# First mixer of a two-block transformer: order by hand up to the queries, compression before the decays, its additions on GpSimd

## Chip, core and metric

The kernel runs on one core of a Trainium2 chip. The metric is the device time of the whole program in microseconds; the time before is the median of three runs. TensorE is called PE, VectorE DVE, ScalarE ACT, GpSimd POOL, and SyncE, whose queue carries most DMAs, SP.

## The reference, cut to what matters

```python
def reference(x, ...):                       # x [1, 256, 1024] float32
    x = first_block(x, ...)
    return second_block(x, ...)

def first_block(x, ...):                     # one layer
    z = rms_norm(h, attn_norm) @ w_in        # 2856 columns
    nq, nkv, ngate, gq, gk, gv, glr, gout = split(z)
    o_nsa = nsa_mixer(nq, nkv, ngate, ...)   # 8 heads of 64, 2 key groups
    o_gla = gla_mixer(gq, gk, gv, glr, gout, ...)   # 4 heads, keys 64, values 128
    h = h + concat([o_nsa, o_gla]) @ w_out
    u = causal_dwconv(rms_norm(h, ffn_norm) @ w_up, conv_w, conv_b)
    gate, up = split(u)                      # 2816 each
    return h + (silu(gate) * up) @ w_down

def compress(t, pe, w1, w2):                 # in nsa_mixer, for keys and for values
    tb = t[:, blk] + pe[:, None, :]          # 15 blocks of 32 tokens, a new one every 16
    return gelu(tb.reshape(..., 32 * 64) @ w1) @ w2

# nsa_mixer: o = g0 * attention over the 15 compressed blocks
#              + g1 * attention over the selected blocks + g2 * attention in a window
# gla_mixer: linear attention with decay: log_a = log_sigmoid(glr @ w_gate2 + b) / 16,
#            q * exp(b), k * exp(-b), states carried over 4 chunks of 64 tokens,
#            rms_norm(o) * silu(gout)

def second_block(x, ...):                    # conv and attention mixer, then
    h = h + hier_moe(rmsnorm(h, norm2_g), w_group, w_router, w1, w3, w2)
                                             # 64 experts of 1024 x 512, two for each token
```

All operands are float32. The change touches only the first mixer (`nsa_mixer`, `gla_mixer` and the products by `w_in` that feed them) and the load of the router's weights.

## The kernel before

**Products.** PE has no fast float32 product, so each float32 matrix is split in two parts: `split` copies it into a rounded hi part (ACT, L154) and subtracts this from the original for the lo part (DVE, L155). A product is then three matmuls per piece: hi by hi, lo by hi, hi by lo. `tokmm` (L278) gives tokens by columns from pieces of 128 rows by 512 columns, `featmm` (L288) columns by tokens. Both take x turned, multiplied by the norm's gain and split (`gained_T`: transposes by PE at L241, xh by ACT at L246, xl by DVE at L247). The norm's factor per token, `rstd_of` (ACT L258, then small DVE steps of a Newton iteration at L220 to L222), is multiplied in behind the products.

**Weights.** `load_raw` (L122) brings them by SP in blocks of 1 MB into four raw buffers used in rotation, the halves of `low_61` and `low_62`; `load_k` makes two blocks of 512 columns, `load_c` one of 256. A raw buffer is loaded again when its last reader is done: the splits, and for the compression's weights, which are used as they are, PE. The split parts go through six pairs of buffers.

**Stages, in the program's order.** x is loaded (L187) between the two halves of the columns `w_cmp` that feed the compression (L181), turned, and multiplied by `w_cmp` (into cT), `w_q` (48 matmuls at L278, into qg), `w_kv` (48, into kg and vv), `w_gg` (the gates, 24 small ones), `w_gqk` (96, into qt and kt_), `w_gv` (48) and, later, `w_go` (48). Between them stand small chains: `gl` (DVE L383, the gate input) goes through a small product at L399, an exponential and a logarithm (ACT L401 to L403) and a running sum (PE L409) to the decays `e0`, `e1`, `e2` (ACT, and POOL at L419 and L422), which DVE multiplies into qt, kdT (L466) and kt_.

**Compression.** `sel`, eight matmuls at L502, spreads cT over partitions; ACT copies the result to `cd`; sixteen additions of 64x8x15 elements (DVE L510) add the position weights and write `tb`; 128 small matmuls (L518) multiply `tb` by `cmp_w1`; then a GELU, a transpose (L523), small products by `w2c` (L531, L534), and for the keys a norm and a rotation on DVE (`kcd`, L554). In the program it stands behind the decays and the loads of `w_gv`.

**The attention.** From L650 on: three score products for each of four head pairs (L654, L667), row maxima (DVE L627), exponentials (ACT), scalings (DVE L635), turned blocks (PE L641) and products by the values (L662, L675). PE's other products fill its waits.

**What sets the order.** A planner orders each engine's instructions; each engine then works in that order, and waits where an operand is missing. `tc.manual_schedule` keeps the written order instead, for the engines named. PSUM has three buffers for products (`pf`), two small ones (`pc`), two for transposes (`pt`) and one more (`po`).

**Later stages.** From 176 us a gated feed-forward layer with convolution, then the second block's mixer; from about 600 us the experts' weights, 402 MB, stream through buffers while PE multiplies them.

## Time and profile before

| | |
|---|---|
| median of three runs | 1534.73 us (1533.23 to 1536.35) |
| the profiled execution | 1533.03 us, of it the span 1531.2 us; mean granted clock 0.943 |
| busy in the span | PE 88%, DVE 39%, ACT 27%, POOL 8% |
| chain that ended last | DMA 50%, PE 44%, DVE 3% |
| moved | 502 MB, 328 GB/s over the span |

The profile is of one execution. Its timeline has a line for each run of like instructions: when they start, how long they take together, the engine, the line of the program, what is written and read, and in brackets how long the engine stood idle before and what it waited for. A view by stretches adds busy times between two moments. The chain that ended last is followed back from the last instruction to whatever released each step.

### The profile page before, as it was taken

To read this page: it belongs to the slowest core of one execution; us is meant where nothing else is said; L and a number is where in the kernel's file an instruction comes from. 1 tells how busy PE (TensorE), PEld (TensorE's weight loads), DVE (VectorE), ACT (ScalarE), POOL (GpSimd) and SP (SyncE) were. 2 spreads that over 40 slices of the span, in tenths; PEclk is the share of its full clock that TensorE was granted. 3 is DMA by queue.
4 is the path that set the end of the run, shared out by engine and by line. 5 is a ranking of instruction groups with operands and counts; after the bars stand their busy time and mean duration, and the time that the engine had idled before them with its cause. 6 is when DMAs were issued, how large, how long until landed. Compare 5 with 4: busy or idle time off the path is not lost.

```text
span 1531.2 us, 24384 instructions
## 1 busy us (share of the span) xinstructions
PE 1353.7 (88%) x10353; PEld 882.5 (58%) x10353; DVE 601.7 (39%) x1309; ACT 413.4 (27%) x734; POOL 126.8 (8%) x126
## 2 busy tenths in 40 slices
PE   7999999999999998999888888897887888887886
PEld 6766899998899996544343333343333433433332
DVE  5787777767876555322121121211211211111111
ACT  5455666555555443111001000010100000010001
POOL 3100032221212222000000000000000000000000
PEclk9999999999999999999898998988988899889998
DMA  9351666553545568999999999999999999999996
GB/s 322 127 189 56 206 207 216 170 193 121 172 159 202 184 237 345 396 424 426 426 427 426 427 427 425 427 425 427 427 427 427 425 428 425 428 426 426 426 425 246
DMA packets 113376, 502.39 MB, mean 328 GB/s; under 512 B 9825, under 2 KB 70770, under 8 KB 86002
## 3 DMA queue, kind: packets, MB, share of 16 engines
q1 hardware_dynamic: 110322, 499.66, 81.4%
q8 instruction: 83, 1.36, 0.4%
q10 hardware_dynamic: 2944, 1.16, 0.3%
q14 instruction: 27, 0.22, 0.0%
HBM read 499.74 MB, written 1.05 MB: 327 GB/s over the span
## 4 chain that ended last, share of the span: by engine, by line
DMA 50%; PE 44%; DVE 3%; SPq 1%; ACT 1%; issue 1%; POOL 0%; DVEq 0%; ACTq 0%
DMA w<-in_w 28%; DMA low<-in_w 21%; PE pf L288 11%; PE pf L870 8%; PE ps L1278 5%; PE pf L278 5%; PE acc L859 4%; PE oacc L1310 3%; PE ps L1300 1%; DMA low<-in_w_in 1%; PE acc L278 1%; PE ps L1211 1%; PE pc L1033 0%; PE pc L1010 0%; PE oacc L1315 0%
## 5 line engine op out<-in xcount | busy, mean ns | idle before, releaser
L1278 PE MATMUL ps<-w,xg 128*32 128x256 f32 x2896 | 287.5, 458 | 98.7 <-DMA w<-in_w 97.8
L1278 PEld LDWEIGHTS ps<-w,xg 128*32 128x32 f32 x2896 | 133.1, 130 | 218.0 <-DMA w<-in_w 114.2
L1310 PE MATMUL oacc<-y,swT 128*128 128x512 f32 (+1 forms) x516 | 237.3, 602 | 0.6 <-DVE y L229 0.4
L1289 DVE TENSOR_TENSOR ar<-ps,a 64x128 f32<-64x128 f32 x128 | 48.8, 382 | 443.9 <-ACT a L1284 443.1
L1278 PE MATMUL ps<-low,xg 128*32 128x256 f32 x1200 | 156.6, 481 | 47.0 <-DMA low<-in_w 46.2
L1310 PEld LDWEIGHTS oacc<-y,swT 128*128 128x128 f32 x516 | 92.6, 189 | 119.2 <-issue 117.4
L1284 ACT ACTIVATE a<-ps 64x256 f32<-64x256 f32 x64 | 24.0, 375 | 507.6 <-PE ps L1278 507.6
L229 DVE COPY y<-ps 128x512 f32<-128x512 f32 x64 | 44.3, 692 | 213.8 <-PE ps L1300 213.8
L1278 PEld LDWEIGHTS ps<-low,xg 128*32 128x32 f32 x1200 | 68.9, 136 | 102.2 <-DMA low<-in_w 53.4
L1300 PE MATMUL ps<-w,aT 128*32 128x512 f32 x696 | 86.5, 598 | 1.4 <-issue 1.4
L1262 ACT ACTIVATE swT<-ps 128x256 f32<-128x256 f32 x64 | 24.5, 383 | 211.4 <-PE ps L1260 211.4
L1211 PEld LDWEIGHTS ps<-oh,h3m 128*128 128x128 f32 x512 | 61.0, 195 | 26.7 <-issue 26.7
L1211 PE MATMUL ps<-oh,h3m 128*128 128x128 f32 x512 | 67.1, 285 | 1.0 <-DVE oh L1203 1.0
L227 ACT ACTIVATE y<-ps 128x512 f32<-128x512 f32 (+1 forms) x65 | 38.4, 590 | 108.4 <-PE ps L1300 108.3
L1213 DVE TENSOR_TENSOR xg<-ps,par 128x512 f32<-128x512 f32 x32 | 22.1, 692 | 69.6 <-PE ps L1211 69.6
L901 POOL TENSOR_TENSOR g<-uc,uc 128x256 f32<-128x256 f32 x22 | 31.7, 1439 | 160.2 <-ACT uc L899 151.5
L1300 PEld LDWEIGHTS ps<-w,aT 128*32 128x32 f32 x696 | 18.7, 109 | 40.2 <-issue 33.3
L1300 PE MATMUL ps<-low,aT 128*32 128x512 f32 x312 | 40.4, 598 | 1.0 <-DMA low<-in_w 1.0
L1253 DVE TENSOR_SCALAR sw<-cst,rk,Wm 128x128 f32<-128x128 f32 x128 | 38.1, 340 | 2.3 <-PE ps L1260 2.3
L1260 PEld LDWEIGHTS ps<-ident,sw 128*128 128x128 f32 x128 | 17.9, 141 | 33.5 <-issue 33.5
L155 DVE TENSOR_TENSOR w_downl<-low,w_downh 128x1024 fp32r<-128x1024 f32 x22 | 27.1, 1231 | 24.7 <-ACT w_downh L154 24.7
L859 PE MATMUL acc<-w_downh,gh 128*128 128x512 f32 x88 | 34.9, 397 | 0.0
(536 smaller groups left out, 2289.9 us busy)
## 6 DMA issues: line engine op xcount, KB each, us to landing
w<-in_w SPq DMA_DIRECT2D x119, 2048.0 KB, 39.4
low<-in_w SPq DMA_DIRECT2D x51, 2048.0 KB, 39.4
low<-in_w_in SPq DMA_DIRECT2D x36, 1024.0 KB, 5.0
w<-in_w SPq DMA_DIRECT2D x30, 1024.0 KB, 9.4
low<-in_w_up SPq DMA_DIRECT2D x22, 1024.0 KB, 5.2
low<-in_w SPq DMA_DIRECT2D x12, 1024.0 KB, 10.3
low<-in_w_down SPq DMA_DIRECT2D x11, 1024.0 KB, 5.1
low<-in_w_out SPq DMA_DIRECT2D x4, 1024.0 KB, 7.9
```

The lines of the kernel that those rows point to most:

```text
L227: nc.scalar.activation(o, a, AF.Copy, scale=1.0 if scale is None else scale)
L229: nc.vector.tensor_copy(o, a)
L278: nc.tensor.matmul(o, xp[a][:, k0 + k, t * 128:(t + 1) * 128], wp[b][:, k], start=(first and j == 0 and n == 0), stop=(last and j == len(p ...
L288: nc.tensor.matmul(o, wp[b][:, k], xp[a][:, k], start=(n == 0), stop=(n == 23))
L859: nc.tensor.matmul(acc[2 * t + h], gp[a][:, t * 128:(t + 1) * 128], wd[b_][:, 0, h * 512:(h + 1) * 512], start=(ch == 0 and i == 0), stop= ...
L870: nc.tensor.matmul(pu[:, u * 256:(u + 1) * 256], cur[u][b_][:, k], hp[a][:, k], start=(kh == 0 and u == 0 and i == 0 and k == 0), stop=(i ...
L1211: nc.tensor.matmul(pg[:, k * 128:(k + 1) * 128], h3m[:, t, 4 * k4 + k], oh[:, t].rearrange("p e s -> p (e s)"), start=(t == 0), stop=(t == 1))
L1253: nc.vector.tensor_scalar(sw[:, t], io32[:, None, :].to_broadcast([128, 4, 32]), rk[:, t, e:e + 1], Wm[:, t, e:e + 1], op0=OP.is_equal, op ...
L1278: nc.tensor.matmul(ph[32 * g:32 * g + 32, 0:256].rearrange("p (q x) -> p q x", q=2), xg[:, 4 * k0 + k, 32 * i:32 * i + 32], w13[2 * k0 + u ...
L1289: nc.vector.tensor_mul(ar[64 * q:64 * q + 64].rearrange("p (r j) -> p j r", r=4), ph[64:128, s].rearrange("p (j r) -> p j r", r=4), a[64:1 ...
L1300: nc.tensor.matmul(py[32 * r:32 * r + 32, :n], aT[:, 32 * r:32 * r + 32], w(r), start=True, stop=True, tile_position=(0, 32 * r))
L1310: nc.tensor.matmul(oacc[2 * t + h][:, o:o + n], swT[:, t], y[:, :n], start=(e == 0), stop=(e == NE - 1), skip_group_check=True)
```

## The change

- x and `w_cmp` come in turn, by halves of their rows and columns: x, w_cmp, x, w_cmp. Before, they came as half of w_cmp, x, x, half of w_cmp.
- The gates' columns `w_gg`, `w2c` and the router's weights `wr` are packed into one array on the host side of the inputs, and each is loaded by one DMA in place of two.
- Nine bf16 matmuls of a constant stand before PE's first transposes; their result isn't used.
- From the turning of x to the last q product the order on PE, ACT and DVE is the written one: x's first half is turned and multiplied by w_cmp's first rows (two parts of columns, the second later), then the second half; w_cmp's lo parts are made by DVE, no longer by POOL (L155 there); `rstd_of` stands behind the splits of `w_q`, and the splits of `w_kv` follow.
- The compression stands ahead of kv (sel, cd, tb) and, from its 128 matmuls on, directly behind gqk; the decays' and the rotations' code comes after it.
- The sixteen additions into `tb` are POOL's (L411), no longer DVE's (L510).

```diff
+    w_cmp = raw_tile([128, 8, 256])
     for h in range(2):
         c = slice(h * 512, (h + 1) * 512)
         nc.sync.dma_start(xres[:, :, c], A["x"][:, c].rearrange("(t p) n -> p t n", p=128))
-    raws.append(load_cmp(1))
+        nc.sync.dma_start(w_cmp[:, 4 * h:4 * h + 4], A["w_in"][h * 512:(h + 1) * 512, 512:768].rearrange("(k p) n -> p k n", p=128))
...
-    xp = gained_T(xres, pp("attn_norm"), lambda: firsts.pop(0)())
+    idle = po_("idle")
+    for _ in range(9):
+        nc.tensor.matmul(idle.rearrange("p (r k) -> p r k", r=4), onesb, onesb[:, None, :].to_broadcast([128, 4, 128]),
+                         start=True, stop=True, skip_group_check=True)
...
-    for i in range(2):
-        featmm(pcv[:, i * 256:(i + 1) * 256], split(raws[i], "w_cmp", eng=nc.gpsimd), xp)
-    rstd = rstd_of(xres, h1[:, 1, :512], "n1")
+    wps = []
+
+    def part(h, i):
+        for n, (a, b) in enumerate(((0, 0), (1, 0), (0, 1))):
+            for kk in range(4):
+                nc.tensor.matmul(pcv[:, i * 256:(i + 1) * 256], wps[h][b][:, kk, i * 128:(i + 1) * 128], xp[a][:, 4 * h + kk],
+                                 start=(h == 0 and i == 0 and n == 0 and kk == 0), stop=(h == 1 and n == 2 and kk == 3),
+                                 skip_group_check=True)
+
+    by_hand = ExitStack()
+    by_hand.enter_context(tc.manual_schedule(engines={mybir.EngineType.PE, mybir.EngineType.Activation, mybir.EngineType.DVE}))
+    xp = gained_T(xres, pp("attn_norm"), lambda: firsts.pop(0)(), None, 0)
+    wps.append(split(w_cmp[:, 0:4], "w_cmp"))
+    part(0, 0)
+    gained_T(xres, pp("attn_norm"), lambda: firsts.pop(0)(), xp, 1)
+    wps.append(split(w_cmp[:, 4:8], "w_cmp"))
+    part(0, 1)
+    part(1, 0)
+    part(1, 1)
...
     wq = load_k(w_in, 0, 512, "w_q")
+    rstd = rstd_of(xres, h1[:, 1, :512], "n1")
...
+    nc.sync.dma_start(w_gg.rearrange("p k n -> p (k n)"), packed("w_gg"))
+    wkv = load_k(w_in, 768, 512, "w_kv")
...
+    by_hand.close()
...
-                    nc.vector.tensor_add(tb[q0, i, lo * 8:lo * 8 + 8, g, 0:15], src,
+                    nc.gpsimd.tensor_add(tb[q0, i, lo * 8:lo * 8 + 8, g, 0:15], src,
                                          pe[q0, lo * 8:lo * 8 + 8][:, :, None].to_broadcast([64, 8, 15]))
...
-    nc.scalar.dma_start(wr[:, :, 0:8], A["w_group_2"].rearrange("(k p) n -> p k n", p=128))
-    nc.scalar.dma_start(wr[:, :, 8:72], A["w_router_2"].rearrange("(k p) n -> p k n", p=128))
+    nc.scalar.dma_start(wr.rearrange("p k n -> p (k n)"), packed("wr"))
```

**SP's queue, from the loads of gqk (before: of kv) to those of `w_gv`** (`low_61` and `low_62` are the raw buffers; in_w_in 128x8x256 is gqk, 128x4x512 before is kv, then gv). Before:

```order
L122 DMA low_61<-in_w_in 128x4x512 x2
L122 DMA low_62<-in_w_in 128x8x256 x2
L122 DMA low_61<-in_w_in 128x4x512 x2
L122 DMA low_62<-in_cmp_w_k 128x8x256
L122 DMA low_62<-in_cmp_w_v 128x8x256
L122 DMA low_61<-in_cmp_w_k 128x8x256
L122 DMA low_61<-in_cmp_w_v 128x8x256
L122 DMA low_62<-in_w_in 128x4x512 x2
```

Now:

```order
L130 DMA low_61<-in_w_in 128x8x256
L130 DMA low_62<-in_w_in 128x8x256
L130 DMA low_62<-in_cmp_w_k 128x8x256
L130 DMA low_61<-in_cmp_w_v 128x8x256
L130 DMA low_61<-in_cmp_w_k 128x8x256
L130 DMA low_62<-in_cmp_w_v 128x8x256
L130 DMA low_62<-in_w_in 128x4x512
L130 DMA low_61<-in_w_in 128x4x512 x2
```

The two loads of `w_gv` stood ahead of the compression's weights; they now stand behind them, into the same buffers.

**PE from the end of gqk to the compression.** Before:

```order
L288 MATMUL pf<-xh,w_gqkl 128x256 x4
L502 MATMUL pc<-cT,sel 128x256 x4
L472 MATMUL pt<-ident,kdT 128x128 x4
L482 MATMUL pt<-ident,qg 128x128 x4
L278 MATMUL pf<-w_gvh,xh 128x512
L486 MATMUL pt<-ident,low_63 128x128 x4
L482 MATMUL pt<-ident,qg 128x128 x4
L518 MATMUL po<-low_62,tb 32x128 x2
...
L518 MATMUL po<-low_62,tb 32x128 x30
L518 MATMUL po<-low_61,tb 32x128 x32
```

Now:

```order
L297 MATMUL pf<-xh,w_gqkl 128x256 x4
L488 MATMUL po<-low_62,tb 32x128 x2
L488 MATMUL po<-low_61,tb 32x128 x2
...
L493 MATMUL pt<-ident,hid 128x128
L501 MATMUL pc<-w2c,hidT 32x64 x2
L504 MATMUL pc<-w2c,hv 128x64 x2
L287 MATMUL pf<-w_gvh,xh 128x512 x2
L287 MATMUL pf<-w_gvh,xl 128x512 x2
L287 MATMUL pf<-w_gvh,xh 128x512 x2
```

The 128 matmuls by `tb` now follow gqk, and the first products by `w_gv` come behind the compression's small ones; the transposes of kdT, qg and the keys (L472, L482, L486 before) stand later, among the products by `w_gv`.

**DVE up to gl, and POOL's additions.** DVE before:

```order
L155 TENSOR_TENSOR w_kvl<-low_61,w_kvh 128x1024
L355 TENSOR_TENSOR cT<-pf,rrow_310 128x512
L360 SCALAR_TENSOR_TENSOR qg<-pf,n1y,row 128x512
L155 TENSOR_TENSOR w_gqkl<-low_62,w_gqkh 128x1024 x3
L448 TENSOR_REDUCE qss<-low_63 128x16
...
L155 TENSOR_TENSOR w_gvl<-low_61,w_gvh 128x1024
...
L374 SCALAR_TENSOR_TENSOR kg<-pf,n1y,row 128x128 x2
...
L383 TENSOR_TENSOR gl<-pc,rrow_310 16x256
```

DVE now:

```order
L385 TENSOR_TENSOR cT<-pf,rrow_342 128x512
...
L553 TENSOR_TENSOR qg<-qg,qry 128x1024
L163 TENSOR_TENSOR w_gqkl<-low_62,w_gqkh 128x1024
L541 TENSOR_TENSOR rqa<-qg,cst 128x256
L542 TENSOR_TENSOR rqb<-qg,cst 128x16x8
L543 TENSOR_TENSOR rqb<-qg,cst 128x16x8
L544 TENSOR_TENSOR qg<-rqa,rqb 128x16x16
L422 SCALAR_TENSOR_TENSOR kg<-pf,n1y,row 128x128 x4
...
L431 TENSOR_TENSOR gl<-pc,rrow_342 16x256
```

POOL now:

```order
L376 TENSOR_SCALAR negb<-cst 128x128
L377 CAST cmpb<-cst 128x32
L378 CAST beforeb<-cst 128x128
L411 TENSOR_TENSOR tb<-cd,par 64x8x15 x16
L467 TENSOR_TENSOR e_794<-bT 128x512
L470 TENSOR_TENSOR e_789<-e_789,rrow_342 128x512
```

The splits of `w_gv` have left the rows ahead of gl, q's scaling and rotation have come in; POOL's sixteen additions stand ahead of its steps for the decays.

## Rows read from the trace of the kernel before

**Rows 1.** The page's part 4: the chain that ended last, share of the span by engine.
```profile
DMA 50%; PE 44%; DVE 3%; SPq 1%; ACT 1%; issue 1%; POOL 0%; DVEq 0%; ACTq 0%
```

**Rows 2.** Stretches: from:to, length, busy (xinstructions) of PE, PEld, DVE, ACT, POOL; clock; DMA; GB/s.
```profile
176.00:600.00 424.00, 421.90 (x2999) 396.31 (x2999) 286.22 (x449) 224.22 (x337) 103.62 (x96) 1.00 0.58 197
600.00:1531.20 931.20, 772.03 (x6318) 362.66 (x6316) 189.56 (x532) 91.89 (x204) 1.03 (x1) 0.91 0.99 417
59.60:86.60 27.00, 21.51 (x219) 16.70 (x218) 18.29 (x44) 11.98 (x19) 4.28 (x4) 1.00 0.52 189
101.20:137.00 35.80, 34.97 (x238) 21.85 (x236) 25.90 (x82) 23.75 (x71) 2.50 (x2) 1.00 0.18 58
7.00:9.00 2.00, 1.75 (x9) 1.78 (x10) 0.12 (x1) 1.35 (x4) 1.55 (x1) 1.00 1.12 340
725.70:729.30 3.60, 3.53 (x60) 1.95 (x60) 0.00 (x0) 0.00 (x0) 0.00 (x0) 1.00 1.02 432
740.90:743.00 2.10, 2.04 (x24) 1.12 (x28) 0.00 (x0) 0.00 (x0) 0.00 (x0) 0.57 0.99 421
```

**Rows 3.** Timeline, start: start us, us, engine line op out<-in xcount [idle before <-releaser].
```profile
5.07 1.06 ACT L154 ACTIVATE w_cmph<-low 128x1024 fp32r<-128x1024 f32 x1 [2.10 <-DMA low<-in_w_in]
7.25 1.09 PE L241 MATMUL pf<-ident,low 128*128 128x128 f32 x4 [7.25 <-DMA low<-in_x]
17.25 0.63 PE L278 MATMUL pf<-w_qh,xh 128*128 128x512 f32 x2
```

**Rows 4.** The kv products in the chain that ended last; PE's sel products in the timeline.
```profile
30.24 11.22 PE pf L278 x48
57.76 1.89 PE L502 MATMUL pc<-cT,sel 128*128 128x256 f32 x8
```

**Rows 5.** Timeline of DVE beside the kv products, up to gl and behind it.
```profile
30.10 1.22 DVE L155 TENSOR_TENSOR w_kvl<-low,w_kvh 128x1024 fp32r<-128x1024 f32 x1
...
39.42 1.23 DVE L155 TENSOR_TENSOR w_gvl<-low,w_gvh 128x1024 fp32r<-128x1024 f32 x1 [0.26 <-ACT w_gvh L154]
...
40.65 0.61 DVE L374 SCALAR_TENSOR_TENSOR kg<-pf,n1y,row 128x128 f32<-128x128 f32 x2
...
43.99 0.42 DVE L383 TENSOR_TENSOR gl<-pc,rrow 16x256 f32<-16x256 f32 x1
...
45.37 1.20 DVE L454 TENSOR_TENSOR qg<-qg,qry 128x1024 f32<-128x1024 f32 x1
...
46.67 0.41 DVE L442 TENSOR_TENSOR rqa<-qg,cst 128x256 f32<-128x256 f32 x1
```

**Rows 6.** Timeline of POOL and, beside its operation at 185.63, of DVE.
```profile
4.88 0.85 POOL L496 COPY sel<-ident 64x64 f32<-64x64 f32 x4
...
185.63 1.62 POOL L901 TENSOR_TENSOR g<-uc,uc 128x256 f32<-128x256 f32 x1 [56.57 <-ACT uc L899]
...
196.28 0.74 POOL L901 TENSOR_TENSOR g<-uc,uc 128x256 f32<-128x256 f32 x1 [2.35 <-DVE uc L897]
...
186.56 0.97 DVE L896 SCALAR_TENSOR_TENSOR uc<-v,par,uc 128x255 f32<-128x255 f32 x1
188.22 0.57 DVE L896 SCALAR_TENSOR_TENSOR uc<-v,par,uc 128x255 f32<-128x255 f32 x1 [0.70 <-ACT uc L895]
```

**Rows 7.** Timeline of PE and DVE, 59.6 to 86.6 us; the page's loads of w_in.
```profile
61.02 0.66 PE L472 MATMUL pt<-ident,kdT 128*128 128x128 f32 x4 [1.36 <-DVE kdT L466]
...
70.12 3.69 PE L518 MATMUL po<-low,tb 128*32 128x128 f32 x124 [1.07 <-DVE tb L510]
...
86.55 0.70 PE L278 MATMUL pf<-w_goh,xh 128*128 128x512 f32 x2 [0.87 <-DVE st L617]
...
60.88 2.87 DVE L510 TENSOR_TENSOR tb<-cd,par 64x120 f32<-64x120 f32 x6
...
low<-in_w_in SPq DMA_DIRECT2D x36, 1024.0 KB, 5.0
```

**Rows 8.** Timeline of PE among the experts.
```profile
740.96 5.33 PE L1278 MATMUL ps<-w,xg 128*32 128x256 f32 x60 [3.30 <-DMA w<-in_w]
```

More of the change, by code (lines that the diff above doesn't have):

```diff
@@ L73 @@
 PCOLS = _o
+for _k, _n in (("w_gg", 8 * 48), ("w2c", 2 * 2 * 64), ("wr", 8 * 72)):
+    PLAY[_k] = (_o, _n)
+    _o += _n
 RLAY, _o = {}, 0
@@ L207, in block_kernel @@
     onesb = consts.tile([128, 128], BF, name="onesb")
+    nc.gpsimd.memset(onesb, 1.0)
     def rsqrt_mean(ss, n, width, name):
@@ new lines, in block_kernel @@
+    pk = pc_()
+    for h in range(2):
+        nc.tensor.matmul(pk[:32, 0:64], hidT[:, 0, h], w2c[:, 0, h], start=(h == 0), stop=(h == 1))
+    pv = pc_()
+    for h in range(2):
+        nc.tensor.matmul(pv[:, 0:64], hv[:, h], w2c[:, 1, h], start=(h == 0), stop=(h == 1))
+    vc = mix.tile([128, 8, 64], F32, name="vc")
+    vr = small.tile([128, 64], F32, name="vr", bufs=1)
+    nc.scalar.activation(vr, pv[:, 0:64], AF.Copy)
+    nc.gpsimd.tensor_mul(vc, vr[:, None, :].to_broadcast([128, 8, 64]),
+                         cc("hmask")[:, :, None].to_broadcast([128, 8, 64]))
@@ L434, in block_kernel @@
+    kct = small.tile([128, 2, 16], F32, name="kct")
+    nc.vector.tensor_copy(kct.rearrange("p a b -> p (a b)"), pt[:, :32])
+    for a in range(2):
+        nc.vector.tensor_scalar(kcT[:, :, a], kct, cc("bmask")[:, a:a + 1], None, op0=OP.mult)
     gv = h1[:, 0].rearrange("p (t v) -> p t v", t=2)
```

155 lines of the change are left out of this document (69 added, 86 removed).

## Prediction

> **What bounds the kernel now.** I read the chain that ended last first. By engine it is half DMA and 44% PE [rows 1]: two regimes. The busy times by stretch show where each holds [rows 2]. From 600 us to the end DMA is at 0.99, while PE is busy 772.03 of 931.20 us: that part takes what the expert weights take to come. From 176 to 600 us PE is busy 421.90 of 424.00, so no operand is missed there. The change touches only what lies before 176 us (and, for the router's weights, two small loads on ACT's queue that become one; costed at nothing: they are ahead of their reader in a stretch in which PE is full, and with that cover gone one transfer fewer still isn't a loss). Behind 176 us nothing has slack that could swallow a shift: PE is full, and then the expert transfers, which start when buffers of the dense part come free, run back to back. So a microsecond gained or lost before 176 us arrives at the end as a microsecond, and the question is what PE waits for in these 176 us.
>
> The same view gives the two stretches with waits: 59.6 to 86.6 us (27.00 long, PE busy 21.51, so 5.5 of waits) and the attention, 101.2 to 137.0 us (34.97 of 35.80, so 0.8). The reader should see in [rows 7] whose waits the 5.5 are: kdT, tb and st, all made by DVE, which before and during the products by the compression's weights does the sixteen additions (six of them 2.87 us).
>
> **The start.** x and the compression's weights now come in turn by halves. Before, the first 0.5 MB is in use at 5.07 us and PE starts when all of x is there, at 7.25 [rows 3]. Now the first 0.5 MB is half of x: PE can start at about 5.0, 2.2 earlier. That isn't kept whole. The table by hand sets the second half's transposes behind the first products by w_cmp, and the last of these need DVE's lo part, so each half is a chain: two groups of transposes (1.09 each), a hi split (1.06), a lo split (1.23 [rows 5]), in sum about 4.5, twice 9.0. With the gained copies and the products that nothing covers, some 2 us by the rest of the old path (10.0 from 7.25 to the first q product at 17.25 [rows 3]), q starts near 16.0: **-1.2**. Bounds: 0 if the second half's chain eats all, -2.2 if nothing is eaten. The q and the kv products behind keep their distance, since in both orders kv waits for DVE to empty q's PSUM. The four gate products that filled this wait come later; that is about 0.5 and inside the bounds. The nine idle products run while PE has nothing to do and cost nothing; the granted clock was 1.00 from 7 us on [rows 2], so there is no clock for them to win. The splits of w_kv come before rstd now and are out of the way earlier.
>
> **The additions on GpSimd.** They need the sel products, which stand behind the first eight kv products, and so run beside the rest of kv, where DVE works towards gl (the gate input that PE's next small product waits for, in order, with all of gqk behind it). From 30.10 to gl at 43.99 DVE spent 13.9 us [rows 5]. Out of this go one w_kv and two w_gv splits (3 x 1.23 = 3.7) and the four kg products that run behind the last kv product anyway (2 x 0.61 = 1.2); in come q's scaling (1.20) and its rope (four steps of at most 0.41, 1.6): 11.8. PE gives it 11.22 for kv plus 1.89 for the eight sel products that now stand there [rows 4]: 13.1, a slack of 1.3. What one addition takes on GpSimd no row shows. The nearest are a copy of 64 columns (0.85 for four, 0.21 each) and an operation on 256 columns with two SBUF operands undisturbed (0.74) [rows 6]; for 120 columns I go between them in proportion, 0.37, sixteen of them 5.9. What they cost DVE shows where the 0.74 operation meets DVE's: it takes 1.62, and DVE's 255-column operation beside it 0.97, not 0.57 [rows 6]. DVE so loses 0.40 for each 0.74 of GpSimd's work, 0.54 of it: 5.9 x 0.54 = 3.2, less the slack: **+1.9**. Bounds: 0 if the additions fall in pauses, 4.6 (5.9 - 1.3) if each shuts DVE out for its whole length. [...]
>
> **The compression ahead of gv.** Its 128 products (3.69 for 124 in [rows 7]) follow gqk with their operands long made, so the waits for kdT and tb (1.36 and 1.07 in the rows) go. What is late next is w_gv: SP has it behind the compression's weights, and its buffer is theirs. Its first transfer can start when half of the products have read, 1.85 after they began; it takes 5.0 (the median of such loads [rows 7]) and a hi split of 1.06: 7.9 and some 0.1 of hand-over. PE has 3.7 of products and about 1.0 of small ones (hid, w2c) until then, and waits 3.3. After that kcd is due: its chain of some twenty small DVE steps has w_gv splits of 1.23 between them, about 1.0 late; a transposing buffer 0.7 and the copies of gv 0.8 (as the 0.87 for st at 86.55). These three are estimates by the like waits of [rows 7]. Together 5.8 in place of 5.5: **+0.3**. Bounds: -2.2 (only the 3.3 remains) and +2.5 (a second w_gv half waits as long as st's and kdT's together, 2.2 more).
>
> **The attention.** go's 48 products are its fillers now and end behind its last product, where before most of them ran ahead. Two more w_out splits stand on DVE between its row maxima and scalings, which the turned blocks on PE wait for: 2 x 1.23. DVE goes from 25.90 of 35.80 to 28.4 (0.79). I take the two whole, **+2.4**, because DVE's share was lower still (18.29 of 27.00) where PE waited 5.5 us for it [rows 2]. Bounds: 0 if the pauses take them, 4.9 if the two others that ran early come in as well.
>
> **Sum:** -1.2 + 1.9 + 0.3 + 2.4 = +3.4. Against the profiled execution (1533.03, of it 1531.2 span) that is 1536.4. This execution lies 1.7 below the median of the runs, 1534.73, so on the median: 1538.1.
>
> **Rivals.**
> *The additions are free.* They fall where DVE waits for PE, and GpSimd's term is 0: +1.5, 1536.2. For it: GpSimd has nothing else to do there, so the adds may take their time. Against: the slack is 1.3, not 5.9. Chance 0.27.
> *Faster: DVE was the pace from 59.6 to 86.6.* All sixteen additions (6 take 2.87, so 16 take 7.7) leave a stretch where DVE is busy 18.29 us. If PE then finds kcd, the transposing buffer and gv's copies ready, of the 5.5 only the 3.3 for w_gv is left, -2.2; with nothing lost beside kv or in the attention: -1.2 - 2.2 = -3.4, 1531.3. It decides once the waits for kcd and the copies are under 0.5 together and the attention's stay at 0.8. For it speaks that each wait named at present ends with DVE; against, that four w_gv splits (4.9) enter the same stretch. Chance 0.20.
> *Slower still: the clock.* [...] Chance 0.15.
> My forecast itself: 0.38.
>
> **Numbers.** A measurement of this kernel can tell 0.2%, 3.1 us, from no change, so faster means under 1531.7 and slower over 1537.8. Faster: three quarters of the second rival (0.15) and 0.03 from the first. Slower: the clock (0.15), 0.24 of my forecast, which is just over the line, and 0.03 from the first. The rest, 0.40, is the same: 0.21 of the first rival, 0.05 of the second, 0.14 of the forecast. The likeliest case by itself spans 1536 to 1540.5. The range takes in the faster rival and the clock with part of their bounds: 1530.5 to 1542.5; all upper bounds at once (4.6 + 2.5 + 4.9) lie outside.
>
> **What would show it.** Start: first q product near 16.0 (17.25 before). GpSimd: sixteen additions of about 0.4 between 32 and 42 us, and a wait of PE for gl of about 2 at the small gate product. Compression: no wait for tb, then about 3.3 for w_gv, at a granted clock of 1.00 behind it. Attention: some 3 us of waits in all, at the turned blocks. The forecast is wrong if PE comes to the up projection's steady run (176 us now) earlier than that, or more than 7 us later.

## The result and the profile after

The changed kernel takes **1544.66 us** (median of 4 runs, 1543.19 to 1546.26) against 1535.34 us (1533.23 to 1536.35) on the same chip: ratio **1.0067 [1.0054, 1.0079]**, about 10 us slower. The forecast was 3.4 us slower and its range ended at 1542.5: the direction was right, the size three times too small. The profiled execution after took 1543.19 us (span 1541.2), against 1533.03 (span 1531.2), so the two traces differ by 10.0 us in the span.

The stretches of the kernel after, columns as in [rows 2]:

```profile
33.00:52.40 19.40, 16.24 (x87) 13.83 (x86) 17.78 (x37) 5.93 (x10) 8.79 (x16) 1.00 0.55 178
52.40:59.00 6.60, 6.60 (x36) 5.77 (x36) 3.60 (x15) 5.08 (x8) 0.00 (x0) 0.74 0.01 2
67.20:75.40 8.20, 5.17 (x139) 4.34 (x137) 2.56 (x10) 3.56 (x8) 1.00 (x2) 0.97 0.65 223
101.00:137.00 36.00, 35.86 (x232) 21.63 (x231) 27.65 (x82) 23.09 (x78) 0.00 (x0) 1.00 0.18 59
176.00:600.00 424.00, 421.00 (x3016) 396.74 (x3016) 291.19 (x464) 225.36 (x339) 101.11 (x94) 1.00 0.57 196
```

The two regimes of the kernel before are still there. The attention has lost its waits (35.86 of 36.00). Beside the start, the new losses stand in the first two rows: 3.16 us of PE's time are missing beside kv, and behind that the granted clock is 0.74 over 6.6 us: 0.53 from 54.20 to 57.80, where four gqk products take 1.05.

PE's timeline after, the rows that answer to [rows 3], [rows 4] and [rows 7]:

```profile
1.01 4.02 PE L328 MATMUL idle<-onesb 128*128 128x512 bf16 x9 [1.01 <-POOL onesb L216]
4.83 1.09 PE L250 MATMUL pf<-ident,low 128*128 128x128 f32 x4
...
10.36 1.22 PE L338 MATMUL pf<-xh,w_cmph 128*128 128x256 f32 x4 [3.59 <-ACT w_cmph L162]
...
17.83 0.74 PE L338 MATMUL pf<-xh,w_cmph 128*128 128x256 f32 x4 [2.08 <-ACT w_cmph L162]
...
21.10 0.63 PE L287 MATMUL pf<-w_qh,xh 128*128 128x512 f32 x2
...
52.32 0.69 PE L447 MATMUL po<-wg,gl 17*128 17x256 f32 x2 [3.16 <-DVE gl L431]
...
55.00 1.05 PE L297 MATMUL pf<-xh,w_gqkh 128*128 128x256 f32 x4
...
58.17 0.64 PE L297 MATMUL pf<-xl,w_gqkh 128*128 128x256 f32 x4
...
67.27 3.70 PE L488 MATMUL po<-low,tb 128*32 128x128 f32 x128
...
75.41 1.22 PE L287 MATMUL pf<-w_gvh,xh 128*128 128x512 f32 x2 [2.19 <-ACT w_gvh L162]
```

Four long waits stand here, two of them in the start. Of the five short ones of the kernel before, four were for kdT, tb and st (1.36, 1.20, 1.07 and 0.87); all of these are gone. The fifth was 0.91 for `low`, which ACT makes, and is 0.19 now (PE's timeline before):

```profile
83.69 1.99 PE L609 MATMUL pf<-low,kdk 64*128 64x256 f32 x12 [0.91 <-ACT low L601]
```

Three of the four long waits are followed by rows that are too long: four products by w_cmp take 1.22 at 10.36 us and 0.64 later, four gqk products 1.05 at 55.00 and 0.64 later, two gv products 1.22 at 75.41 and 0.62 later. The first is no clean case: the turns ahead of it, at 4.83, were as slow (1.09).

The up projection's steady run is the group of 120 products in the chain that ended last, before and after:

```profile
176.09 14.39 PE pf L870 x120
183.82 14.39 PE pf L897 x120
```

These are products of split parts. What a float32 product takes on PE unsplit, the experts show in the trace before: each one by `y` (L1310, 128x512) stands there as two records, and eight records, four products, take 3.70 us at 1503.88, 0.9 for one. Three products of split parts of that shape take 0.7 (six by `w_q` from 17.25 to 18.64).

The ledger, from PE's rows in both traces (kv is here its first product by `w_kv`; the end of gqk is the start of the products by tb, before the change with the eight sel products behind it):

| stretch | before | after | difference | forecast |
|---|---|---|---|---|
| to the first q product | 17.25 | 21.10 | +3.85 | -1.2 |
| from there to kv | 12.99 | 11.68 | -1.31 | 0 |
| kv to the end of gqk, sel counted in both | 29.41 | 34.49 | +5.1 | +1.9 |
| from there to the steady run | 116.44 | 116.55 | +0.1 | +2.7 |
| from there to the span's end | 1355.1 | 1357.4 | +2.3 | 0 |

DVE and POOL beside kv, after (they answer to [rows 5] and [rows 6]):

```profile
36.49 9.20 POOL L411 TENSOR_TENSOR tb<-cd,par 64x120 f32<-64x120 f32 x16 [12.65 <-ACT cd L405]
...
41.63 0.38 DVE L230 SCALAR_TENSOR_TENSOR qrt<-qrt,qrv 128x16 f32<-128x16 f32 x1
42.05 0.47 DVE L231 SCALAR_TENSOR_TENSOR qry<-qrt,qry 128x16 f32<-128x16 f32 x1
...
43.86 1.51 DVE L553 TENSOR_TENSOR qg<-qg,qry 128x1024 f32<-128x1024 f32 x1
...
49.92 0.68 DVE L550 TENSOR_REDUCE kss<-ksqq 128x8 f32<-128x512 f32 x1
50.63 0.17 DVE L223 TENSOR_SCALAR krv<-kss 128x8 f32<-128x8 f32 x1
...
51.85 0.42 DVE L431 TENSOR_TENSOR gl<-pc,rrow 16x256 f32<-16x256 f32 x1
```

An addition takes 0.575 us on POOL, and while they run DVE's steps on 16 columns take 0.37 to 0.48 (0.17 in the run below that has the additions on DVE; those on 8 columns take 0.17 once POOL is done), its scaling of q 1.51 (1.20 in [rows 5]). gl comes 7.9 us later than before.

### The profile page after: what moved, and what is told of

It is laid out like the page before. It is cut to its first block, busy times and chain, and to the rows that moved or that the text cites. A ratio compares the mean times of both kernels' runs of the same rounds, so it can differ in the third digit from the quotient of the medians.

```text
span 1541.2 us, 24404 instructions
## 1 busy us (share of the span) xinstructions
PE 1356.3 (88%) x10362; PEld 883.6 (57%) x10362; DVE 604.2 (39%) x1295; ACT 410.6 (27%) x732; POOL 130.1 (8%) x139
## 3 DMA queue, kind: packets, MB, share of 16 engines
q8 instruction: 83, 1.36, 0.4%
HBM read 499.78 MB, written 1.05 MB: 325 GB/s over the span
## 4 chain that ended last, share of the span: by engine, by line
DMA 52%; PE 42%; DVE 3%; ACT 1%; issue 1%; POOL 0%; ACTq 0%; SPq 0%; DVEq 0%
DMA w<-in_w 33%; DMA low<-in_w 18%; PE pf L297 11%; PE pf L897 8%; PE pf L287 5%; PE acc L886 4%; PE ps L1304 3%; PE oacc L1336 2%; PE ps L1326 1%; PE acc L287 1%; PE ps L1237 1%; DMA low<-in_w_in 1%; PE pc L1060 0%; PE pc L1037 0%; PE oacc L1341 0%
## 5 line engine op out<-in xcount | busy, mean ns | idle before, releaser
L1304 PE MATMUL ps<-w,xg 128*32 128x256 f32 x2896 | 280.8, 448 | 104.5 <-DMA w<-in_w 103.6
L1304 PEld LDWEIGHTS ps<-w,xg 128*32 128x32 f32 x2896 | 129.9, 128 | 222.3 <-DMA w<-in_w 118.2
L1310 ACT ACTIVATE a<-ps 64x256 f32<-64x256 f32 x64 | 24.0, 375 | 510.1 <-PE ps L1304 510.1
L1304 PEld LDWEIGHTS ps<-low,xg 128*32 128x32 f32 x1200 | 68.0, 135 | 102.8 <-DMA low<-in_w 55.3
```

The source lines that it names most:

```text
L1304: nc.tensor.matmul(ph[32 * g:32 * g + 32, 0:256].rearrange("p (q x) -> p q x", q=2), xg[:, 4 * k0 + k, 32 * i:32 * i + 32], w13[2 * k0 + u ...
```

## Experiments

Three questions were open: which part of the change costs what, whether the additions' engine or their place hurts, and whether the rest of the change is worth anything. Each ratio is to runs of the kernel before on the same chip, taken beside the run.

**Raw buffers.** The change keeps w_cmp in one raw buffer instead of two, so every later load goes one buffer further, and SP's first loads of experts into raw halves are issued at 589.37 us, not at 576.66, while the up projection came only 7.7 later. This could explain the last line of the ledger.

```diff
+    n_raw[0] += 1
```

> The changed kernel with one step more of the counter that picks the raw buffer, put in at the end of the first mixer, so that the later loads use the same halves as in the kernel before. Theory: the change loads w_cmp into one raw buffer where two were used, so every later load sits one buffer further; the last loads of w_o then lie in the halves that the first expert loads want, and these start 2.1 to 2.8 us later than the shift of the dense part explains. Then the steady run of the up projection stays near 183.8, the first loads of experts into the raw buffers come 7.9 (not 12.7) after those of the kernel before, and the time is about 2 us under the changed kernel's (about 1542.5). Rival: the 2.1 us behind 600 us are variation of the expert stream from run to run; then the time stays at 1544.7 within a microsecond.

Measured: 1544.9 us, 1.0073 [1.0056, 1.009]. SP's expert loads into raw halves are issued at 586.30 us, 3.1 earlier, and the time is unmoved: the theory isn't borne out, though two medians of four runs can't quite exclude its 2 us. From the steady run to the span's end this trace has 1355.7 us, as the theory has it. But the steady run itself is at 185.58, 1.8 later than in the changed kernel's trace, and up to there the two are one program. They part behind the wait for gl, where PE starts at half speed here and at full speed there (0.69 at 52.32):

```profile
52.48 1.22 PE L447 MATMUL po<-wg,gl 17*128 17x256 f32 x2 [3.06 <-DVE gl L431]
```

So a steady run read from one trace can lie 2 us off by the clock alone. And over the fourteen traces of this study that distance lies between 1355.0 and 1358.8, with either use of the buffers, and the page's rate from 600 to 1500 us between 422 and 424 GB/s; one part in 424 of 930 us is 2.2 us. So the +2.3 of the ledger's last line is within what this stretch varies by.

**The start undone**, the rest of the change kept (x whole between the halves of w_cmp, no written order, no idle products, two raw buffers).

```diff
-    w_cmp = raw_tile([128, 8, 256])
+    raws = [load_cmp(0)]
...
+    raws.append(load_cmp(1))
...
-    by_hand.enter_context(...)
...
+    xp = gained_T(xres, pp("attn_norm"), lambda: firsts.pop(0)())
+    for i in range(2):
+        featmm(pcv[:, i * 256:(i + 1) * 256], split(raws[i], "w_cmp", eng=nc.gpsimd), xp)
```

> The changed kernel with the start of the kernel before: w_cmp by halves of its columns around x, x turned at once, w_cmp's lo parts on GpSimd, rstd at its old place, no order by hand, no idle products; the packed loads, the early compression and the additions on GpSimd stay. Two raw buffers are used for w_cmp again. Theory: the start by hand costs 2.5 us at the first kv product (32.8 against 30.2); that comes back, and with the raw buffers the 2 us at the experts: about 1540. The wait for gl and the low clock behind it stay (3 us and 1.6). Rival: the start's delay is swallowed by the wait for gl, which DVE sets; then the product by gl comes at 52 as in the changed kernel and only the 2 us of the buffers are won, 1542.5.

Measured: 1540.62 us, 1.0042 [1.0028, 1.0056]; q at 16.92, kv at 28.36. So the new start costs about 4 us (3.8 by the two ratios; their intervals together leave some 1 to 7). The trace has 4.2 at q, 4.4 at kv and 3.9 at the product by gl, but only 0.9 at the steady run (182.88). The wait for gl is as long as in the changed kernel or a little longer, and behind it, as behind the wait for w_gv, half speed lasts longer (PE's timeline):

```profile
48.39 1.22 PE L431 MATMUL po<-wg,gl 17*128 17x256 f32 x2 [3.50 <-DVE gl L415]
...
54.45 0.98 PE L302 MATMUL pf<-xh,w_gqkl 128*128 128x256 f32 x4
...
73.08 1.22 PE L292 MATMUL pf<-w_gvh,xh 128*128 128x512 f32 x2 [2.29 <-ACT w_gvh L162]
```

Seven groups of two gv products are slow here, four in the changed kernel. The rest of the 4 us lies behind the steady run in these two traces (1355.0 us against 1357.4), in the stretch that varies.

**Twelve of the sixteen additions left out.** This run leaves out that part of the computation (tb stays zero there).

```diff
-                    nc.gpsimd.tensor_add(tb[...], src, pe[...])
+                    if lo == 0 and h == 0:
+                        nc.gpsimd.tensor_add(tb[...], src, pe[...])
```

> The changed kernel with four of the sixteen additions; the other twelve are left out, so that parts of tb stay zero. Theory: the additions on GpSimd hold the small DVE steps up beside them (0.37 to 0.48 each in place of 0.17), so gl is late by 3.2 us and the clock falls behind this wait. Without twelve of them the small steps beside the kv products take 0.17 to 0.2, PE waits under 0.7 us for gl, the clock stays at 1.00, the products by gqk end near 62.5 (67.2) and the up projection's steady run begins near 179: time 4 to 5 us under the changed kernel, 1540. Rival: DVE's own order (q's scaling and rotation and k's norm now ahead of gl) makes gl late; then the wait for gl stays over 2 us.

Measured: 1540.14 us, 1.0038 [1.0023, 1.0052]. PE's wait for gl is gone (0.17), and with it the low clock there (view by stretches):

```profile
33.00:50.00 17.00, 16.83 (x91) 14.22 (x89) 15.38 (x38) 6.52 (x11) 1.70 (x4) 1.00 0.70 218
50.00:63.40 13.40, 13.40 (x107) 12.44 (x107) 6.76 (x18) 7.68 (x12) 4.37 (x4) 1.00 0.00 1
```

From the first Newton step to gl DVE needs 11.5 us here (37.99 to 49.47) and 14.4 in the changed kernel (37.41 to 51.85): twelve additions on another engine cost DVE 3.0 us.

**The additions on DVE**, in the place that the change gives them.

```diff
-                    nc.gpsimd.tensor_add(tb[q0, i, lo * 8:lo * 8 + 8, g, 0:15], src,
+                    nc.vector.tensor_add(tb[q0, i, lo * 8:lo * 8 + 8, g, 0:15], src,
```

> The changed kernel with the sixteen additions on DVE again, at their new place ahead of kv's end. Theory: on GpSimd they hold DVE's small steps up by some 4 us in 9.2; on DVE they cost it 16 x 0.48 = 7.7 of its own time, but the planner, which now sees DVE's load, puts gl ahead of k's Newton steps and part of the rotation (some 2 us): the wait for gl stays at 3 to 5 us and the time within 2 us of the changed kernel's 1544.7. Rival: the place on GpSimd is the fault, and with DVE doing them the wait falls under 1.5 us and the time by over 3 us.

Measured: 1543.51 us, 1.0058 [1.0041, 1.0075], against 1.0067 with POOL: the intervals overlap. DVE takes 5.18 us for all sixteen in one piece, its small steps are back at 0.17, the planner puts gl ahead of some of k's Newton steps, and gl starts at 51.53 instead of 51.85 (DVE's timeline below); PE waits 2.41 us for it. The engine of the additions is worth next to nothing here; that they stand ahead of gl is what costs.

```profile
36.78 5.18 DVE L411 TENSOR_TENSOR tb<-cd,par 64x120 f32<-64x120 f32 x16 [0.24 <-ACT cd L405]
...
51.53 0.42 DVE L431 TENSOR_TENSOR gl<-pc,rrow 16x256 f32<-16x256 f32 x1
```

**gl's product later.** PE's order by hand, with the product that reads gl behind 48 of the gqk products.

```diff
+    by_hand.enter_context(tc.manual_schedule(engines={mybir.EngineType.PE}))
+    wqk = [load_c(w_in, 1304, 256, "w_gqk"), load_c(w_in, 1560, 256, "w_gqk")]
+    for f in range(2):
+        featmm(pqk[0][:, f * 256:(f + 1) * 256], wqk[0][f], xp)
...
+    featmm(pqk[1][:, 0:256], wqk[1][0], xp)
```

> The changed kernel with PE's order written by hand from the gates' products to the end of gqk: the product by gl stands behind the first 48 gqk products (6 in the changed kernel), the transposes of gr with it, the running sum behind the next 24. Theory: the wait for gl and the low clock behind it are the whole price of the additions' place; with 48 products in between PE comes to gl at about 54, when it is there, waits for nothing, the clock stays at 1.00, and the compression's products start near 62.5 (67.3): the time falls by 4 to 6 us to about 1539.5. Rival: the wait moves on, to the running sum (la is made by ACT and DVE five us after gl's product) or to kdT: then the compression's products start after 65.

Measured: 1542.31 us, 1.005 [1.0033, 1.0067]. The wait for gl is gone, and a wait of 2.16 us for la (what DVE makes of that product) stands in its place at 60.95 us, with its own stretch at half clock (PE's timeline):

```profile
60.95 1.16 PE L467 MATMUL po<-cst,la 128*128 128x128 f32 x8 [2.16 <-DVE la L461]
...
62.58 1.05 PE L297 MATMUL pf<-xl,w_gqkh 128*128 128x256 f32 x4
```

So PE's order isn't the cause either: DVE's chain is late, and PE meets it in one place or the next.

**The start, two attempts to mend it.** First all of x is turned before the first product; then, besides, ACT's table is loaded at the very start and the copies xh and xl alternate between two PSUM tiles.

```diff
-    wps.append(split(w_cmp[:, 0:4], "w_cmp"))
-    part(0, 0)
     gained_T(xres, pp("attn_norm"), lambda: firsts.pop(0)(), xp, 1)
+    wps.append(split(w_cmp[:, 0:4], "w_cmp"))
+    part(0, 0)
```

> The changed kernel with all of x turned first, then both splits of w_cmp, then its four parts; loads as in the change. Theory: in the written order the second half's transposes stand behind the first products, and xh, xl and the splits of the second half behind them, which makes a chain of two halves and lets PE stand for 3.6 and 2.1 us, with the clock at 0.50 after the first. With the turning first the first q product comes near 17.5 (21.1). Behind it the wait for gl takes some of it back or not: if DVE's way to gl starts with the end of q, the time falls by 3 to 4 us. Rival: the loads are what is late (w_cmp's halves in packets of 1 KB, seven us to land); then q starts at 20 or later.

Measured: 1544.78 us, 1.0071 [1.0054, 1.0087], q at 21.33. PE now waits 2.05 us for x's second half and 3.27 for w_cmp: the order of the turns isn't what makes the start late.

```diff
+    warm = small.tile([128, 8], F32, name="warm", bufs=1)
+    nc.scalar.activation(warm, onesb[:, :8], AF.Copy)
...
+        for k, k2 in [(k, k2) for k in range(2) for k2 in k2s] if src is xres else [(k, k2) for k2 in k2s for k in range(2)]:
```

> As e4 (all of x turned first), and in addition one tiny activation ahead of everything, so that ACT loads its table while x is on its way, and xh, xl in turn over the two PSUM tiles of a half (pf, pc, pf, pc), so that no xh follows the xl of its own tile at once. Theory after e4: what makes the start late is, first, the table load behind the gains (1.28 us at 5.1 us in the changed kernel, at 1.7 in the kernel before), second, four waits of 0.55 us of an xh for the xl of the same PSUM tile, third, the clock at half behind PE's wait for w_cmp (some 2 us in e4). Then xh and xl are done near 10.5 (12.9 in e4) and q starts at 18.5 or earlier (21.3). Rival: PE's wait for the second half of x and the loads of w_cmp set it: q stays above 20.

Measured: 1545.22 us, 1.0064 [1.0048, 1.0081], with q at 19.54, 1.8 us earlier than with the turns alone; neither side had that number. ACT's timeline at the changed kernel's start shows what was mended:

```profile
5.14 1.28 ACT L255 ACT_TABLE_LOAD   x1 [5.14 <-DMA par<-in_par]
6.44 0.47 ACT L255 ACTIVATE xh<-pf,par 128x256 fp32r<-128x256 f32 x1
7.46 0.47 ACT L255 ACTIVATE xh<-pf,par 128x256 fp32r<-128x256 f32 x1 [0.55 <-DVE xl L256]
```

The written order puts ACT's table load behind the DMA of par, and the second xh of a PSUM tile waits until DVE's xl has read that tile. What still holds q back is the clock (PE's timeline of the mended start):

```profile
11.59 1.23 PE L349 MATMUL pf<-xh,w_cmph 128*128 128x256 f32 x4 [2.54 <-ACT w_cmph L162]
...
16.68 0.64 PE L349 MATMUL pf<-xh,w_cmph 128*128 128x256 f32 x4
```

The first 24 products by w_cmp take 5.09 us, the last 24 take 2.86. At full speed q would come some 2.2 earlier, by an estimate from these rows, near the 17.25 of the kernel before.

Yet the time didn't fall at all. The product by gl comes at 50.97, 1.35 earlier than in the changed kernel (its wait is 3.35 us), but half speed begins at once behind it (two products by gl in 1.22), and the compression's products start where they did (67.25 against 67.27); the steady run is at 185.19. So this earlier start, which left the long waits in place, was lost to the half clock behind them.

**The idle products left out.**

```diff
-    for _ in range(9):
-        nc.tensor.matmul(idle.rearrange("p (r k) -> p r k", r=4), onesb, onesb[:, None, :].to_broadcast([128, 4, 128]),
-                         start=True, stop=True, skip_group_check=True)
```

> The changed kernel without the nine idle products at its start. Theory: the half clock behind PE's wait of 3.59 us at 10.36 us comes from that wait alone; without the idle products the granted clock there stays near 0.50, the first q product stays at 21.1 us (within 0.3) and the time at 1544 to 1546 us. Rival: the early products make PE's first stretch one that the wait can end, as before the change, where PE did nothing at all for 7.25 us and then ran at 1.00; without them the twelve products at 10.4 us take 1.3 us and not 2.72, q comes near 19.7 us, and the time falls by up to 1.4 us.

Measured: 1546.26 us, 1.0074 [1.0059, 1.009], q at 21.51. Neither side had it right, because both read the clock from its column. In the view by stretches (columns as in [rows 2]) the clock is 1.00 in all of this start:

```profile
11.00:12.00 1.00, 1.00 (x7) 1.00 (x6) 0.69 (x1) 0.00 (x0) 0.00 (x0) 1.00 1.06 391
```

PE's timeline of the same run says otherwise:

```profile
13.22 1.05 PE L250 MATMUL pt<-ident,low 128*128 128x128 f32 x4
14.07 1.06 PE L250 MATMUL pc<-ident,low 128*128 128x128 f32 x4
```

Four turns in 1.05 us are half speed (0.66 for the same shape in [rows 7]), up to about 16 us; in the changed kernel the turns at 13.08 and 13.71 already take 0.80 and 0.60. With the idle products the slow start ended earlier. The column of this run shows 1.00 in every stretch from 0 to 50 us and has its first lower value at 50 to 56 (0.82), so it doesn't tell the speed of this start.

**The packed loads alone**, on the kernel before (with w_kv asked for ahead of two small loads).

```diff
-    nc.sync.dma_start(w_gg[:, :, 0:24], w_in[:, 1280:1304].rearrange("(k p) n -> p k n", p=128))
-    nc.sync.dma_start(w_gg[:, :, 32:48], w_in[:, 2328:2344].rearrange("(k p) n -> p k n", p=128))
+    nc.sync.dma_start(w_gg.rearrange("p k n -> p (k n)"), packed("w_gg"))
+    wkv = load_k(w_in, 768, 512, "w_kv")
```

> The kernel before with nothing but the packed loads: w_gg, w2c and the router's weights by one transfer each, w_kv asked for ahead of the small ones and of cst; start, compression and additions stay as before. Theory: in e2 the first kv product came at 28.4 (30.2 before), since w_kv's splits no longer hold DVE up when q is done; this part of the change is a gain of up to 1.9 us: about 1533.5. Rival: DVE paces the stretch behind (its waits for kdT, tb and st), so that it is given back and the time stays at 1535.

Measured: 1534.18 us, 0.9994 [0.9985, 1.0004]: no difference that can be told. The steady run starts 1.5 us earlier (174.56), of which 0.7 is x, in use at 6.58 us and not at 7.25, though its loads are the same. The interval reaches from 2.3 us faster to 0.6 slower, so whether the 1.5 arrive can't be told.

**The additions behind gl.** The start of the kernel before, the additions on POOL, held back by a tiny copy of gl on POOL ahead of them.

```diff
+    gate = small.tile([16, 8], F32, name="gate", bufs=1)
+    with tc.manual_schedule(engines={mybir.EngineType.Pool}):
+        nc.gpsimd.tensor_copy(gate, gl[:16, :8])
+        for i, pe, cd in cds:
...
+                        nc.gpsimd.tensor_add(tb[q0, i, lo * 8:lo * 8 + 8, g, 0:15], src,
```

> The changed kernel with the start and the two load buffers of the kernel before, and with the sixteen additions on GpSimd held back behind gl (a tiny copy of gl on GpSimd stands ahead of them). Theory: it is the place of the additions beside DVE's chain to gl, not their engine, that makes PE wait for gl; here gl is ready by about 44.5 us with a wait of PE under 0.6 us, the granted clock stays at 1.00 there, the additions run from about 43 to 53 us, the products that read tb stand at 58 to 60.5 us with no wait, the wait for w_gv of about 2.2 us stays, the up projection's steady run starts at 177 to 179 us, the span ends 1355 us behind that: 1534 to 1537 us, 0.999 to 1.001 of before. Rival: the additions hurt wherever they meet DVE; then la and the later steps are late, tb is waited for by over 1 us or the products by tb come after 62 us, the steady run starts after 180 us and the time is over 1538 us.

Measured: **1534.57 us, 0.9998 [0.9989, 1.0007]**, 11 runs. Timeline of POOL:

```profile
45.49 7.92 POOL L423 TENSOR_TENSOR tb<-cd,par 64x120 f32<-64x120 f32 x16
```

and of PE:

```profile
45.32 0.69 PE L437 MATMUL po<-wg,gl 17*128 17x256 f32 x2 [0.37 <-DVE gl L410]
...
58.77 3.70 PE L478 MATMUL po<-low,tb 128*32 128x128 f32 x128
...
66.99 0.73 PE L292 MATMUL pf<-w_gvh,xh 128*128 128x512 f32 x2 [2.27 <-ACT w_gvh L162]
```

The theory holds but for two numbers that cancel: the steady run comes sooner (175.58, not 177 or later), and the span's end is 1357.9 us behind it, not 1355. Against the run with the start undone, only the place of the additions differs: 1540.62 to 1534.57, **6 us** (6.8 by the two ratios, 7.3 at the steady run). With the 4 us of the start (1544.66 to 1540.62) this makes up the 10, as nearly as the ratios can tell. The rest of the change (the packed loads, the compression ahead of gv) is in this run, and in sum it lies between 1.7 us faster and 1.1 slower.

**The wait for w_gv filled.** On top of that, PE's order by hand behind gqk: the turns of kd, q and k ahead of the first product by w_gv, kcd's turn later.

```diff
+    by_hand = ExitStack()
+    by_hand.enter_context(tc.manual_schedule(engines={mybir.EngineType.PE}))
...
-    pt = pt_()
-    nc.tensor.transpose(pt[:, :128], kcd.rearrange("p a b -> p (a b)"), ident)
...
+    by_hand.close()
+    pt = pt_()
+    nc.tensor.transpose(pt[:, :128], kcd.rearrange("p a b -> p (a b)"), ident)
```

> The run of the late additions, and PE's order written by hand between gqk and gv so that the turns of kd, q and k stand between compression's products and the first product by w_gv, and kcd's turn later. Theory: the wait for w_gv is a transfer that can only start when compression's products have read its buffer, so it can be filled but not shortened; with about 2 us of other products in it the wait falls under 1 us, the clock behind it stays at 1.00 and the steady run starts 1 to 3 us earlier than in the run of the late additions, the time is 1531 to 1535 us, at or under the kernel before. Rival: the copies out of PSUM that the turns need stand on DVE and ScalarE ahead of the splits of w_gv, gv's products come as late as before or the attention waits for kcd's turn, and the time is that of the late additions within 0.7 us.

Measured: **1531.65 us, 0.9977 [0.9968, 0.9986]**, faster than both kernels. PE's timeline behind compression's products:

```profile
64.72 0.61 PE L555 MATMUL pt<-ident,kdT 128*128 128x128 f32 x4
65.17 0.60 PE L565 MATMUL pt<-ident,qg 128*128 128x128 f32 x4
67.22 0.73 PE L292 MATMUL pf<-w_gvh,xh 128*128 128x512 f32 x2 [1.45 <-ACT w_gvh L162]
```

The wait falls from 2.27 to 1.45, less than expected, but the clock stays at 1.00 behind it, and eight turns are out of the way. The first gv product is no earlier (67.22 against 66.99): as the theory says, the wait was filled, and the transfer came no sooner. The steady run starts at 172.37, 3.2 earlier; a wait of 0.72 for kcd is what is left there.

**Idle products at that start**, fourteen of them ahead of x.

```diff
+    idle = po_("idle")
+    with tc.manual_schedule(engines={mybir.EngineType.PE}):
+        for _ in range(14):
+            nc.tensor.matmul(idle.rearrange("p (r k) -> p r k", r=4), onesb, onesb[:, None, :].to_broadcast([128, 4, 128]),
```

> The run with the filled wait, and fourteen idle products on PE ahead of the first turn of x, so that PE is busy from about 1.0 us until x is there at 7.2 us. Theory: PE starts at half clock whatever the granted clock's row says there (four turns take 0.85 us to the next four before the change and 0.45 us later in the kernel), and work done before x comes brings the full clock earlier; the sixteen turns of x then take about 2.0 us and not 3.4, the first q product stands at 15.8 to 16.5 us (17.15 without), of which kv keeps at least half, and the time is 0.4 to 1.4 us under that of the run with the filled wait. Rival: ScalarE, which is busy without a pause from 9 to 18 us with its copies and splits, sets the start: the turns are faster, but q stays within 0.3 us of 17.15 and the time is the same. Second rival: idle products don't raise the clock (they ran for 4 us at half speed in the changed kernel); the turns keep 0.85 us for each four, and nothing changes.

Measured: 1531.27 us, 0.9976 [0.9966, 0.9986], the same as without them. PE's timeline from the start:

```profile
1.01 5.43 PE L334 MATMUL idle<-onesb 128*128 128x512 bf16 x14 [1.01 <-POOL onesb L221]
7.21 0.63 PE L255 MATMUL pf<-ident,low 128*128 128x128 f32 x4 [0.77 <-DMA low<-in_x]
...
12.22 0.75 PE L302 MATMUL pf<-xh,w_cmph 128*128 128x256 f32 x3 [0.52 <-ACT xh L260]
...
66.90 1.15 PE L292 MATMUL pf<-w_gvh,xh 128*128 128x512 f32 x2 [1.58 <-ACT w_gvh L162]
```

The turns are at full speed now (0.63 for four, not 1.09), so the idle products did raise the clock here. But PE then waits for ACT's xh, and q comes only 0.44 earlier (16.71). The first rival had the cause: ACT, which is busy without a pause from 9 to 18 us (9.00 of 9.00 in the run of the late additions, with the same start but for the idle products), sets this start. The product by gl is still 0.44 earlier (45.05 against 45.49), but behind the wait for w_gv PE is at half speed here, to 70.7 us, where it wasn't without the idle products, and the steady run is 0.3 later (172.70). Nothing can be seen in the time.

## Why the prediction was wrong

By its own sign the forecast was wrong: the steady run came 7.7 us later, and it allowed 7. Three of its steps failed.

**The start (-1.2) failed, in sign too: +3.85 at q, +2.5 at kv.** The forecast gave each half's chain 4.5 us and everything else 2, in sum 11 from x's first half to q. The trace has 16.3: 5.5 to the first product (ACT's table load of 1.28 behind par and the 0.55 waits for a shared PSUM tile were not in the sum), 2.7 for twelve products at half speed, 4.8 from there to the last 24, and 3.3 for those. The forecast let 36 products hide in 2 us, though its own order has them between the chains. Of the 1.3 that came back from q to kv, 0.84 is kv's wait for q's PSUM, gone with the splits of w_kv put earlier; the other 0.5 are four gate products that stand behind kv now and only moved to the ledger's next line. Undoing the start brought 3.8 us by the ratios.

**"No clock for the idle products to win" failed.** It rested on the 1.00 for 7 to 9 us in [rows 2], while the first turns in [rows 3] take 1.09 for four and the same shape in [rows 7] takes 0.66. The duration was right and the column was not. What followed from it was right by luck: the idle products are worth 0.4 us at q here, and nothing in the time behind a start that ACT sets.

**The additions (+1.9) were mis-sized: +4.6**, the 5.1 of the ledger less the gate products. Two parts of the term failed. The slack was put at 1.3, and is about 0.3: with four additions PE still waits 0.17 for gl (49.94), though by the rows of that run they cost DVE only some 0.4 (two small steps at 0.40 and 0.38, not 0.17). K's sum of squares and six Newton steps (0.68 and 6 times 0.2) have moved ahead of gl on DVE as well, which the forecast didn't count. And a wait of 3.16 us isn't paid once: behind it twenty gqk products take 3.9 us (54.28 to 58.17) and not 2.4, 1.5 more. What the additions cost DVE, 3.2 in the forecast, came out right by luck: 3.0 for twelve and some 0.4 for four, but from additions of 0.575 us each and not 0.37, 9.2 in all, of which DVE lost a third and more and not 0.54.

That the term came out at 4.6, its upper bound, is luck: 3.1 of it is PE's wait for gl and 1.5 the clock behind it. The bound took it that each addition shuts DVE out for its whole length, and no run shows that: beside 9.2 us of additions DVE lost some 3.4, its steps on 16 columns take 0.37 to 0.48 in place of 0.17, and its split at 40.05 takes 1.21 in the midst of them, as at 35.03 ahead of them. What makes the small steps longer no run here singles out. The run with the additions on DVE shows that it isn't the heart of the matter: with no addition on GpSimd gl was late all the same (51.53).

**Compression ahead of gv (+0.3) and the attention (+2.4): in sum +0.1.** The waits for kdT, tb and st went, as said (5.5 us of waits by DVE were 4.5; 0.91 was ACT's). The wait for w_gv came, 2.19 and not 3.3; the small waits for hid and hidT (0.42, 0.38) took the place of the estimated ones for kcd and the copies. Half clock behind it (four groups of two gv products in 1.22, 1.05, 1.05 and 0.71, at full clock 0.62) cost about 1.4: the lower clock, which the forecast has among its slower cases, did come, and behind the wait for gl as well. The attention's term failed outright: DVE's share rose to 0.77 (27.65 of 36.00), nearly as forecast, and PE had no wait worth the name (35.86 of 36.00). A busier DVE was no wait here, with other products of PE ahead of the turned blocks. A loss that the forecast had no term for came in their place: ahead of the steady run, from 164 us on, PE's waits add up to 2.1 us (the longest 1.03 for xh), where before they came to 1.2.

Half speed behind a long wait stands in these traces: behind 3.30 us at 740.96 before the change (60 products in 5.33 at 0.57, against 3.53 at 1.00 [rows 2, 8]), and in the changed kernel behind 3.16 and 2.19 us (four gqk products in 1.05, two gv products in 1.22). Full speed follows 1.36 for kdT (four turns in 0.66), 1.45 in the run with the wait filled (two gv products in 0.73) and, at 17.83, 2.08 (four products in 0.74). So the length of the wait alone doesn't tell the cases apart: half speed also follows 2.05 us in the run with all of x turned first (four turns in 1.11) and 1.58 in the run with fourteen idle products (two gv products in 1.15). The forecast's 0.15 for the clock was the author's estimate, and no run shows such a chance; what the runs show in its place is 1.5 us behind the wait for gl and 1.4 behind the one for w_gv. The clock belonged into the sum, with a chance, in each place where a long wait was forecast.

**"A microsecond before 176 us arrives as a microsecond"** held within what can be seen: 10 us in the ratio, 7.7 at the steady run, and the last 2.3 within what the transfers' stretch varies by. Over all thirteen kernels that were compared with the one before, the difference by ratio lies from 0.4 us under to 2.6 over the shift of the steady run. The cause of the 2.3 wasn't settled; the raw buffers' run doesn't bear them out as one.

**The rivals.** "The additions are free" fell (3.0 us of DVE for twelve of them, and PE waits for it). "Faster" had its reason right in the main: four of the five waits in 59.6 to 86.6 us ended with DVE, and they did go. To be paid it takes the old start, the additions behind gl and w_gv's wait filled: 1531.65, where that rival said 1531.3 by another sum, so that the nearness of the two is luck.

## What to carry over

When work is moved off a busy engine, ask first what it now stands ahead of: here sixteen additions cost about 6 us ahead of gl, much the same on either engine, and nothing that can be seen behind it. Price a long wait of PE with the half clock that may follow (1.5 us behind gl here, 1.4 behind w_gv), and fill it rather than shorten it where a transfer sets its end. Don't read 2 us from the steady run of a single trace: one program was 1.8 us apart there in two. Read PE's clock from the duration of one shape in two places, not from the clock's column alone: at this start the column has 1.00 while four turns take 1.09 us, and 0.66 later.

## What the runs showed of the hardware that was not expected

- At the start of the program PE runs at half speed while the clock's column says 1.00: four turns in 1.09 us before the change, 0.63 behind fourteen idle products, which took 5.43 in all. Nine took 4.02 in the changed kernel, and the turns behind them 1.09; with the same start in the raw buffers' run nine took 3.41 and the turns 0.63.
- What follows a like wait differs: behind 3.16 us at 52.32 the first products are at full speed (two by gl in 0.69) and only those from 54.3 to 57.8 at half; behind 3.50 at 48.39 (start undone) the same two take 1.22, and half speed lasts from there to 55.3. It isn't the kernel that makes the difference: the raw buffers' run, the same program up to there, has 1.22 behind 3.06.
- GpSimd's sixteen additions slow DVE's smallest steps (from 0.17 us to between 0.37 and 0.48) far more, in proportion, than its long ones (a split of 1.21 takes 1.21 to 1.47).
- ACT and DVE read one PSUM tile in turn: the second xh waited 0.55 us for xl on the tile, and no longer did when two tiles alternated. Whether the chip or the program's own order of reads makes them take turns, the runs don't tell.
